# Up products of the MLP: the first pass by twos, and sums of token blocks in the order of their products, with a fourth sum buffer

## The chip, the cores and the metric

The kernel runs on one core of one Trainium2 chip. The metric is the device time of one execution in microseconds (us): the median of three runs of the kernel before is 2343.8 us (2342.3 to 2343.92). One more execution was taken with the hardware profiler; all rows of the trace come from it.

## The reference, cut to what matters

A decoder trunk of two layers on 1024 tokens of width 1024, in float32. Each layer has a token mixer (attention in layer 0, a gated recurrence in layer 1) and then a channel mixer. The change is in the first product of the channel mixer, `h @ w1`, in both layers.

```python
D_MODEL = 1024; SEQ = 1024; DEPTH = 2; D_FF = 4 * D_MODEL

def sq_relu_mlp(h, w1, w2):
    a = jax.nn.relu(h @ w1)
    return (a * a) @ w2
...
    for layer in range(DEPTH):
        ...
        h = h + rms_norm(m, norm_gains[layer, 1])
        a = rms_norm(h, norm_gains[layer, 2])
        h = h + rms_norm(sq_relu_mlp(a, mlp_w1[layer], mlp_w2[layer]), norm_gains[layer, 3])
    return h
```

## The kernel before, in words

**Products.** Every float32 factor is split (`split`, L74) into a high half, made by a copy on ACT (L76), and a low half, the remainder, made by a subtraction on DVE (L77). One step of a product is then three matmuls (`mm3`, L81 to L83): high by high, high by low, low by high. The third is the first that reads the low half of the weights. One product of the up stage (`product`) takes 512 of the 1024 features, 128 columns of w1 and 512 tokens: four steps, 12 matmuls.

**The up stage (`mlp_up`).** Features and tokens are cut in two, so the activations are four blocks: B11 and B21 (first 512 tokens; first and second half of the features), B12 and B22 (last 512 tokens). In the code they are `A[0, 0]`, `A[1, 0]`, `A["whole"]` and `A[1, 1]`; in the order of instructions A00, A10, whole (in layer 1 a part of acc) and A11. The 4096 columns of w1 go in 16 blocks p of 256, two halves of 128 each. With a scheme of Strassen's kind a block needs seven products instead of eight. Two are of B11 and B21 and add up in one PSUM bank. The other five (`others`) are, in the order of the code, of T2, T1, T3, B22 and T4, where T1 to T4 are sums of the four blocks: T1 = B12 - B11, T2 = B22 - T1, T3 = B22 - B12, T4 = B21 - T2. Their weights are sums of w1's quarters: wS12 (`w_parts(s12)`; for T2 and T1), wS34 (for T3 and B22), and wb, the plain quarter, for T4.

**The first pass.** For the first eight blocks (`EARLY`) the products of B11 and B21 need only the first 512 tokens. They run while the last tokens still come out of the mixer and are transposed by PE into B12 and B22 (`into_features`, L176). The pass is the loop at L861: weights are loaded and split, B11's product goes to a PSUM bank, ACT copies it out (`first_two`, L805, to a tile he; called sP1), B21's product is added in the same bank (`add_second`), ACT takes relu (L797) and square (L798). sP1 and the result h11 are stored in DRAM by POOL's queue (L865, L794) and loaded again by SP (L875, L877) when `others` reaches the block. There are two banks for this (pool PG, tag mm) and two tiles he.

**The sums.** `tsums` (L726) makes T1 to T4 on DVE in two halves of the features, k = 0 and k = 2. A half has eight sums and four splits, so there are 16 sums and 8 splits of 128x1024 in all; the high half of each split is a copy on ACT. A half needs three buffers s, and there are three. `others` uses two of the same buffers for each block (s12 and s34).

**Results.** Each block adds its products into tiles of 128x512 that rotate through a ring (`h512`): two he, NH of tag h, and NM of tag h2, which lie where `A["whole"]` was, so that they exist only after the sums have read it. A tile comes free when its store to DRAM has landed or its last reader is done. The ring has 13 tiles in layer 0 (NH 7, NM 4) and 14 in layer 1 (NH 4, NM 8).

**Order.** The code is recorded and a scheduler writes each engine's instructions in one fixed order when the program is built; `tc.high_priority(offset=AHEAD[layer])` lets the first pass go ahead of what stands before it in the code. At run time each engine goes through its list and waits for semaphores; nothing overtakes.

Of the kernel before, what the change touches and what calls it, by code (L numbers as in the profile page):

```python
# [11 lines left out]
F32 = mybir.dt.float32  # L12
# [4 lines left out]
ALU = mybir.AluOpType  # L17
# [4 lines left out]
P = 128  # L22
# [17 lines left out]
EARLY = 8  # L40
# [18 lines left out]
def trunk(ctx, tc, x, x_t, positions, norm_gains, mla_w_in, mla_q_norm, mla_kv_norm, mla_w_uq, mla_w_ukv, mla_w_o,  # L59
          hgrn_w_in, hgrn_lb_logits, hgrn_o_norm, hgrn_w_o, mlp_w1, mlp_w2, out):  # L60
    nc = tc.nc
    PE, ACT, DVE, POOL, SP = nc.tensor, nc.scalar, nc.vector, nc.gpsimd, nc.sync

    def pool(stack, name, bufs=1, side=None, **kw):
        return stack.enter_context(tc.tile_pool(name=name, bufs=bufs, side=side, reuse_waits="tile", **kw))
# [3 lines left out]
    def new(p, shape, dt, tag, bufs=None):  # L69
        uid[0] += 1  # L70
        kw = {} if bufs is None else {"bufs": bufs}
        return p.tile(shape, dt, tag=tag, name=f"{tag}_{uid[0]}", **kw)

    def split(dst, src):  # L74

        ACT.activation(dst[:, 0], src, AF.Copy)  # L76
        DVE.tensor_tensor(dst[:, 1], src, dst[:, 0].bitcast(F32), ALU.subtract)  # L77
# [7 lines left out]
    x = x[0]  # L85
# [15 lines left out]
    first = new(const, [P, 1], F32, "first")  # L101
# [523 lines left out]
    q, qstack = mla()  # L625
# [79 lines left out]
    def mlp_up(layer):  # L705
# [3 lines left out]
        w1 = mlp_w1[layer].rearrange("(k p) c -> p k c", p=P)  # L709
        with tc.tile_pool(name=f"up{layer}", bufs=1, side="left", reuse_waits="tile") as wp:  # L710

            NH, NM = (7, 4) if layer == 0 else (4, 8)
            new(wp, [P, 512], F32, "h", NH)
            new(wp, [P, 1024], F32, "s", 3)
            T2 = new(wp, [P, 2, 4, 512], F32R, "T2")
            T3 = new(wp, [P, 2, 4, 512], F32R, "T3")
            T4 = new(wp, [P, 2, 4, 512], F32R, "T4")
# [5 lines left out]
            def f32(x):  # L723
                return x.bitcast(F32)

            def tsums():  # L726

                for k in range(0, 4, 2):
                    def part(X, i):
                        return f32(X[:, i, k:k + 2])  # L730

                    def tmp():
                        return new(wp, [P, 1024], F32, "s", 3).rearrange("p (k c) -> p k c", c=512)

                    a, b, c = tmp(), tmp(), tmp()

                    b12 = B12[:, :, k:k + 2].rearrange("p t k q -> p k t q")

                    def by_tile(x):
                        return x.rearrange("p k (t q) -> p k t q", q=P)  # L740

                    DVE.tensor_tensor(by_tile(b), b12, by_tile(part(B11, 0)), ALU.subtract)
                    DVE.tensor_tensor(b, b, part(B11, 1), ALU.subtract)
                    d = c
                    DVE.tensor_tensor(d, part(B22, 0), b, ALU.subtract)
                    DVE.tensor_tensor(d, d, part(B22, 1), ALU.add)
                    split(T2[:, :, k:k + 2], d)
                    DVE.tensor_tensor(by_tile(a), by_tile(part(B22, 0)), b12, ALU.subtract)
                    DVE.tensor_tensor(a, a, part(B22, 1), ALU.add)
                    split(T1[:, :, k:k + 2], b)  # L750
                    split(T3[:, :, k:k + 2], a)
                    e = d
                    DVE.tensor_tensor(e, part(B21, 0), d, ALU.subtract)
                    DVE.tensor_tensor(e, e, part(B21, 1), ALU.add)
                    split(T4[:, :, k:k + 2], e)

            def product(ps, w, X, more=False):

# [6 lines left out]

            def h512():
                tag = ring[hs["n"] % len(ring)]
                hs["n"] += 1
                p, bufs = {"he": (G, 2), "h": (wp, NH), "h2": (hs["more"], NM)}[tag]
                return new(p, [P, 512], F32, tag, bufs)  # L770

            def raw_early(p):

                own["n"] += 1
                r = new(G0 if own["n"] % 2 else G, [P, 1024], F32, "raw").rearrange("p (k c) -> p k c", c=P)
                SP.dma_start(r, w1[:, :, p * 256:p * 256 + P])
                return r
# [7 lines left out]
            def w_parts(src):  # L785
                own["w"] = own.get("w", 0) + 1
                w = new(G0, [P, 2, 1024], F32R, "w", 1) if own["w"] % 5 == 0 else new(G, [P, 2, 1024], F32R, "w", 4)
                n = src.shape[1] * src.shape[2]
                v = w[:, :, :n].rearrange("p i (k c) -> p i k c", c=src.shape[2])
                split(v, src)  # L790
                return v
# [8 lines left out]
            def first_two(p, wa):  # L800

                a = new(PG, [P, 512], F32, "mm")
                product(a, wa, B11)
                sP1 = h512() if p >= EARLY else new(G, [P, 512], F32, "he", 2)
                ACT.activation(sP1, a, AF.Copy)  # L805
                return a, sP1

            def add_second(p, a, w12):
                product(a, w12[:, :, :, :P], B21, True)
                h11 = h512() if p >= EARLY else new(G, [P, 512], F32, "he", 2)  # L810
                act2(h11, a)
                spill(0, p, h11)
                return h11

            def others(p, rA, rB, wb, sP1, h11, second=None):
                s12 = new(wp, [P, 1024], F32, "s", 3).rearrange("p (k c) -> p k c", c=256)
                s34 = new(wp, [P, 1024], F32, "s", 3).rearrange("p (k c) -> p k c", c=256)
                DVE.tensor_tensor(s12[:, :, :P], rA[:, :, P:], rB[:, :, P:], ALU.add)
                DVE.tensor_tensor(s12[:, :, P:], s12[:, :, :P], rA[:, :, :P], ALU.subtract)
                wS12 = w_parts(s12)  # L820
                DVE.tensor_tensor(s34[:, :, :P], rA[:, :, :P], rA[:, :, P:], ALU.subtract)
                DVE.tensor_tensor(s34[:, :, P:], rB[:, :, :P], s12[:, :, P:], ALU.subtract)
                b = new(PG, [P, 512], F32, "tr")
                product(b, wS12[:, :, :, P:], T2)
                U = h512()
                DVE.tensor_tensor(U, b, sP1, ALU.add)
                if second is not None:
                    h11 = second()
                wS34 = w_parts(s34)
                c = new(PM, [P, 512], F32, "mm")  # L830
                product(c, wS12[:, :, :, :P], T1)
                X5 = h512()
                DVE.tensor_tensor(X5, c, U, ALU.add)
                d = new(PM, [P, 512], F32, "c")
                product(d, wS34[:, :, :, :P], T3)
                h22 = h512()
                DVE.tensor_tensor(h22, d, X5, ALU.add)
                product(c, wS34[:, :, :, P:], B22, True)
                h12 = X5
                DVE.tensor_tensor(h12, c, U, ALU.add)  # L840
                product(d, wb, T4, True)
                h21 = U
                DVE.tensor_tensor(h21, d, U, ALU.add)
                for h in (h22, h12, h21):
                    act2(h, h)
                spill(3, p, h22)
                s1 = h512()
                DVE.tensor_tensor(s1, h12, h22, ALU.add)
                spill(4, p, s1)
                s2 = h512()  # L850
                DVE.tensor_tensor(s2, s1, h11, ALU.subtract)
                spill(5, p, s2)
                s3 = h12
                DVE.tensor_tensor(s3, h11, h12, ALU.subtract)
                spill(6, p, s3)
                spill(1, p, h21)
                s4 = h512()
                DVE.tensor_tensor(s4, h21, s2, ALU.subtract)
                spill(2, p, s4)

            for p in range(EARLY):  # L861
                with tc.high_priority(offset=AHEAD[layer]):
                    w12 = w_parts(raw_early(p))
                    a, sP1 = first_two(p, w12[:, :, :4])
                    POOL.dma_start(psp[p * P:(p + 1) * P, :], sP1)  # L865
                    add_second(p, a, w12[:, :, 4:])
            tsums()

            act["whole"].close()
            hs["more"] = pool(act["stack"], f"more{layer}", side="right")  # L870
            for p in range(NP):
                rA, rB = raw_half(p, 0), raw_half(p, 1)
                if p < EARLY:
                    h11 = h512()
                    SP.dma_start(h11, hsp[0, p * P:(p + 1) * P, :])  # L875
                    sP1 = h512()
                    SP.dma_start(sP1, psp[p * P:(p + 1) * P, :])  # L877
                    others(p, rA, rB, w_parts(rB[:, :, P:]), sP1, h11)
                else:
                    a, sP1 = first_two(p, w_parts(rA[:, :, :P]))  # L880
                    wb = w_parts(rB)
                    others(p, rA, rB, wb[:, :, :, P:], sP1, None, lambda: add_second(p, a, wb))
# [487 lines left out]
```

## Time and profile before

| | us |
|---|---|
| median of 3 runs | 2343.8 |
| lowest, highest | 2342.3, 2343.92 |
| profiled execution, its own time | 2346.75 |
| span of the profiled execution, first to last instruction | 2345.1 |
| PE busy in it | 2266.8 (97%) |
| DVE, ACT, POOL busy | 1596.5, 1169.4, 346.9 |

The profiled execution took 2.95 us more than the median of the runs. Start times in the rows are from the start of the span. A row of a timeline names the engine, the line, the operation, what it writes and reads, and, where the engine was idle before it, for how long and who ended the idle time. Matmuls overlap: one row of 0.39 us starts some 0.23 us after the one before it, so the pace is read from the starts. PEclk is the granted clock of the tensor engine as a share of full speed.

### The profile page before, as it was taken

The numbers are of one execution on the slowest core, as the hardware profiler recorded it, in microseconds if no ns is written. First come the engines' busy times: TensorE is split into PE (matmuls) and PEld (weight loads), VectorE is DVE, ScalarE is ACT, GpSimd is POOL, SyncE is SP. The second block draws the span as 40 slices with busy tenths as digits, with TensorE's granted clock in tenths as the row PEclk, the third lists the DMA queues.
The fourth block names the chain that finished last, engine by engine and source line by source line (L and its number), as shares of the span: only waits on it lengthen the run. The fifth ranks groups of instructions, "written<-read, shape, count | busy, mean of one in ns | idle before, by whom it ended". The sixth has DMA issues, their size and how long they took to land. (4 is left out here: it accounts for less than half of the span.)

```text
span 2345.1 us, 30698 instructions
## 1 busy us (share of the span) xinstructions
PE 2266.8 (97%) x11487; PEld 1910.8 (81%) x11487; DVE 1596.5 (68%) x2287; ACT 1169.4 (50%) x1893; POOL 346.9 (15%) x718
## 2 busy tenths in 40 slices
PE   8999999989999999999999999999979999999998
PEld 8789998867778878888788888888767788788886
DVE  5658885378766556588655767756778766466696
ACT  5445655364445444445565546755454445444343
POOL 1300000021212100001322213212221222100001
PEclk9999999999999999999999999999999999999999
DMA  7010002465644484565612333222346544663664
GB/s 220 24 32 10 10 10 79 146 211 189 210 157 166 159 299 135 180 229 175 198 46 82 110 102 121 82 81 70 108 165 220 182 164 149 210 240 120 217 216 159
DMA packets 229283, 333.12 MB, mean 142 GB/s; under 512 B 16743, under 2 KB 136590, under 8 KB 229134
## 3 DMA queue, kind: packets, MB, share of 16 engines
q1 hardware_dynamic: 205326, 251.45, 33.4%
q0 software_dynamic: 23808, 79.71, 9.1%
q8 instruction: 90, 1.47, 0.3%
q14 instruction: 59, 0.48, 0.1%
HBM read 247.22 MB, written 83.89 MB: 141 GB/s over the span
## 5 line engine op out<-in xcount | busy, mean ns | idle before, releaser
L77 DVE TENSOR_TENSOR w<-raw,w 128x1024 fp32r<-128x1024 f32 (+1 forms) x240 | 278.1, 1163 | 185.2 <-ACT w L76 184.2
L76 ACT ACTIVATE w<-raw 128x1024 fp32r<-128x1024 f32 (+1 forms) x240 | 237.8, 997 | 239.2 <-PE mm L83 119.6
L81 PE MATMUL mm<-A,w 128*128 128x512 f32 x832 | 331.2, 399 | 23.4 <-ACT he L797 12.2
L82 PE MATMUL mm<-A,w 128*128 128x512 f32 x832 | 327.6, 395 | 0.6 <-DVE A L77 0.6
L76 ACT ACTIVATE w<-s 128x1024 fp32r<-128x1024 f32 x156 | 165.3, 1060 | 321.8 <-PE c L83 118.5
L83 PE MATMUL mm<-A,w 128*128 128x512 f32 x832 | 325.5, 393 | 0.0
L77 DVE TENSOR_TENSOR w<-s,w 128x1024 fp32r<-128x1024 f32 x156 | 190.5, 1222 | 143.9 <-ACT w L76 143.8
L81 PEld LDWEIGHTS mm<-A,w 128*128 128x128 f32 x832 | 157.7, 190 | 64.5 <-ACT he L797 15.7
L145 POOL TENSOR_TENSOR rstd<-rstd,nhalf 128x1 f32<-128x1 f32 x56 | 44.4, 794 | 959.1 <-DVE rstd L144 934.2
L83 PEld LDWEIGHTS mm<-A,w 128*128 128x128 f32 x832 | 157.6, 190 | 33.1
L82 PEld LDWEIGHTS mm<-A,w 128*128 128x128 f32 x832 | 157.8, 190 | 32.2 <-DVE A L77 1.0
L82 PE MATMUL mm<-w,w 128*128 128x512 f32 x432 | 168.7, 391 | 1.0 <-DVE w L77 0.9
L83 PE MATMUL mm<-w,w 128*128 128x512 f32 x432 | 168.3, 390 | 0.0
L81 PE MATMUL mm<-w,w 128*128 128x512 f32 x432 | 154.4, 392 | 3.2 <-ACT u L1015 2.0
L794 POOL DMA_DIRECT2D hsp<-h x177 | 95.4, 540 | 388.8 <-ACT h L798 208.7
L81 PE MATMUL mm<-w,A 128*128 128x256 f32 (+2 forms) x352 | 111.5, 319 | 4.2 <-ACT A L76 3.5
L83 PE MATMUL mm<-w,A 128*128 128x256 f32 (+2 forms) x352 | 110.9, 316 | 0.0
L82 PE MATMUL mm<-w,A 128*128 128x256 f32 (+2 forms) x352 | 110.2, 314 | 0.0
L81 PE MATMUL c<-T,w 128*128 128x512 f32 x256 | 99.6, 389 | 0.0
L82 PE MATMUL c<-T,w 128*128 128x512 f32 x256 | 99.6, 389 | 0.0
L83 PE MATMUL c<-T,w 128*128 128x512 f32 x256 | 99.3, 389 | 0.0
L81 PEld LDWEIGHTS mm<-w,w 128*128 128x128 f32 x432 | 80.8, 188 | 22.6 <-ACT u L1015 2.9
(443 smaller groups left out, 5641.2 us busy)
## 6 DMA issues: line engine op xcount, KB each, us to landing
raw<-in_mlp_w_dram SPq DMA_DIRECT2D x92, 512.0 KB, 4.3
hsp<-h POOLq DMA_DIRECT2D x177, 256.0 KB, 2.9
s<-in_mlp_w_dram SPq DMA_DIRECT2D x80, 512.0 KB, 6.2
raw<-hsp SPq DMA_DIRECT2D x76, 512.0 KB, 4.0
raw<-in_hgrn_w_in_dram SPq DMA_DIRECT2D x64, 512.0 KB, 4.2
sx<-hsp SPq DMA_DIRECT2D x36, 512.0 KB, 3.9
hsp<-he POOLq DMA_DIRECT2D x47, 256.0 KB, 2.8
xt<-in_x_dram SPq DMA_DIRECT2D x16, 512.0 KB, 5.5
```

Of the source, the lines that this page charges most:

```text
L76: ACT.activation(dst[:, 0], src, AF.Copy)
L77: DVE.tensor_tensor(dst[:, 1], src, dst[:, 0].bitcast(F32), ALU.subtract)
L81: PE.matmul(ps, lhs[0], rhs[0], start=start, stop=False, skip_group_check=more)
L82: PE.matmul(ps, lhs[0], rhs[1], start=False, stop=False, skip_group_check=more)
L83: PE.matmul(ps, lhs[1], rhs[0], start=False, stop=stop, skip_group_check=more)
L145: POOL.tensor_tensor(r, r, nhalf[:, :1], ALU.pow)
L794: POOL.dma_start(hsp[i, p * P:(p + 1) * P, :], h)
```

## The change

Three edits in `mlp_up`. The first pass goes by pairs of blocks: both B11 products, then both B21 products. `tsums` is cut in two functions: `tsums12` makes T2 and T1 of both halves, and `tsums34` makes T4 of both halves and then T3 of both; the second is handed to `others` of block 0 as `then` and is recorded between the split of wS12 and the sums of s34. For that the sums of T2 live on, and there is a fourth buffer s; NH is two smaller in both layers, so the ring has 11 and 12 tiles.

```diff
-            NH, NM = (7, 4) if layer == 0 else (4, 8)
+            NH, NM, NS = (5, 4, 4) if layer == 0 else (2, 8, 4)
             new(wp, [P, 512], F32, "h", NH)
-            new(wp, [P, 1024], F32, "s", 3)
+            new(wp, [P, 1024], F32, "s", NS)
...
+            t2s = {}
+
+            def tsums12():
+                for k in (0, 2):
+                    b, d = tmp(), tmp()
+                    DVE.tensor_tensor(by_tile(b), b12(k), by_tile(part(B11, 0, k)), ALU.subtract)
+                    DVE.tensor_tensor(b, b, part(B11, 1, k), ALU.subtract)
+                    DVE.tensor_tensor(d, part(B22, 0, k), b, ALU.subtract)
+                    DVE.tensor_tensor(d, d, part(B22, 1, k), ALU.add)
+                    split(T2[:, :, k:k + 2], d)
+                    split(T1[:, :, k:k + 2], b)
+                    t2s[k] = d
+
+            def tsums34():
+                for k in (0, 2):
+                    e = t2s[k]
+                    DVE.tensor_tensor(e, part(B21, 0, k), e, ALU.subtract)
+                    DVE.tensor_tensor(e, e, part(B21, 1, k), ALU.add)
+                    split(T4[:, :, k:k + 2], e)
+                for k in (0, 2):
+                    a = tmp()
+                    DVE.tensor_tensor(by_tile(a), by_tile(part(B22, 0, k)), b12(k), ALU.subtract)
+                    DVE.tensor_tensor(a, a, part(B22, 1, k), ALU.add)
                     split(T3[:, :, k:k + 2], a)
...
-            def others(p, rA, rB, wb, sP1, h11, second=None):
-                s12 = new(wp, [P, 1024], F32, "s", 3).rearrange("p (k c) -> p k c", c=256)
-                s34 = new(wp, [P, 1024], F32, "s", 3).rearrange("p (k c) -> p k c", c=256)
+            def others(p, rA, rB, wb, sP1, h11, second=None, then=None):
+                s12 = new(wp, [P, 1024], F32, "s", NS).rearrange("p (k c) -> p k c", c=256)
                 DVE.tensor_tensor(s12[:, :, :P], rA[:, :, P:], rB[:, :, P:], ALU.add)
                 DVE.tensor_tensor(s12[:, :, P:], s12[:, :, :P], rA[:, :, :P], ALU.subtract)
                 wS12 = w_parts(s12)
+                if then is not None:
+                    then()
+                s34 = new(wp, [P, 1024], F32, "s", NS).rearrange("p (k c) -> p k c", c=256)
...
-            for p in range(EARLY):
+            for p in range(0, EARLY, 2):
+
                 with tc.high_priority(offset=AHEAD[layer]):
-                    w12 = w_parts(raw_early(p))
-                    a, sP1 = first_two(p, w12[:, :, :4])
-                    POOL.dma_start(psp[p * P:(p + 1) * P, :], sP1)
-                    add_second(p, a, w12[:, :, 4:])
-            tsums()
-
-            act["whole"].close()
-            hs["more"] = pool(act["stack"], f"more{layer}", side="right")
+                    w12, first = {}, {}
+                    for i in (p, p + 1):
+                        w12[i] = w_parts(raw_early(i))
+                        first[i], sP1 = first_two(i, w12[i][:, :, :4])
+                        POOL.dma_start(psp[i * P:(i + 1) * P, :], sP1)
+                    for i in (p, p + 1):
+                        add_second(i, first[i], w12[i][:, :, 4:])
+            tsums12()
+
+            def rest():
+                tsums34()
+
+                act["whole"].close()
+                hs["more"] = pool(act["stack"], f"more{layer}", side="right")
+
...
-                    others(p, rA, rB, w_parts(rB[:, :, P:]), sP1, h11)
+                    others(p, rA, rB, w_parts(rB[:, :, P:]), sP1, h11, then=rest if p == 0 else None)
```

The number of instructions is the same on every engine, and outside the two up stages their order is the same. PE around the last eight transposes of layer 0 (tr_848 and tr_849, which complete B12 and B22), before; mm_871 and mm_881 are the banks of blocks 2 and 4:

```order
L82 MATMUL mm_871_5159<-A10_749_4344,w_870_5156 128x512
L83 MATMUL mm_871_5159<-A10_749_4344,w_870_5156 128x512
L176 MATMUL tr_848_5053<-ident_6_65,y_842_5034 128x128 x4
L176 MATMUL tr_849_5059<-ident_6_65,y_842_5034 128x128 x4
L81 MATMUL mm_881_5233<-A00_748_4343,w_880_5230 128x512
L82 MATMUL mm_881_5233<-A00_748_4343,w_880_5230 128x512
```

The same place on PE after the change; mm_885 is the bank of block 5:

```order
L82 MATMUL mm_885_5254<-A00_748_4343,w_884_5251 128x512
L83 MATMUL mm_885_5254<-A00_748_4343,w_884_5251 128x512
L176 MATMUL tr_848_5053<-ident_6_65,y_842_5034 128x128 x4
L176 MATMUL tr_849_5059<-ident_6_65,y_842_5034 128x128 x4
L81 MATMUL mm_881_5233<-A10_749_4344,w_880_5230 128x512
L82 MATMUL mm_881_5233<-A10_749_4344,w_880_5230 128x512
```

Before, seven products stood ahead of these transposes (B11 of blocks 0 to 3, B21 of 0 to 2); now ten do (B11 of blocks 0 to 5, B21 of 0 to 3). In layer 1 it is nine before and ten now.

ACT in the last third of layer 0's first pass, before (he are sP1 and h11, mm their banks, T1 the high half of a sum):

```order
L805 ACTIVATE he_887_5283<-mm_886_5270 128x512
L798 ACTIVATE he_883_5261<-he_883_5261 128x512
L76 ACTIVATE T1_858_5079<-s_903_5396 128x1024
L797 ACTIVATE he_888_5298<-mm_886_5270 128x512
L805 ACTIVATE he_892_5320<-mm_891_5307 128x512
L798 ACTIVATE he_888_5298<-he_888_5298 128x512
```

And the two last pairs after it; L814 is now the copy, L806 the relu, L807 the square, w_909 is wS12 of block 0:

```order
L814 ACTIVATE he_892_5320<-mm_891_5307 128x512
L76 ACTIVATE T1_858_5079<-s_901_5386 128x1024
L814 ACTIVATE he_896_5341<-mm_895_5328 128x512
L806 ACTIVATE he_897_5356<-mm_891_5307 128x512
L807 ACTIVATE he_897_5356<-he_897_5356 128x512
L76 ACTIVATE T2_854_5075<-s_902_5387 128x1024
L806 ACTIVATE he_898_5372<-mm_895_5328 128x512
L76 ACTIVATE w_909_5410<-s_908_5407 128x1024
```

Before, the copy of a bank, L805, and its relu, L797, stand three places apart, and the copy of the next block's bank follows the relu directly; now the copies of two banks come first and the two relus after them. The high half of wS12 stands behind the last relu.

DVE between the sums and the two weight splits of block 0 in layer 0, before (w_912 is wS12, w_915 is wS34):

```order
L77 TENSOR_TENSOR T3_855_5076<-s_902_5395,T3_855_5076 128x1024
L754 TENSOR_TENSOR s_904_5397<-s_904_5397,A10_749_4344 128x1024
L77 TENSOR_TENSOR w_912_5433<-s_910_5429,w_912_5433 128x1024
L821 TENSOR_TENSOR s_911_5430<-raw_905_5418 128x4x128
L822 TENSOR_TENSOR s_911_5430<-raw_906_5420,s_910_5429 128x4x128
L77 TENSOR_TENSOR T4_856_5077<-s_904_5397,T4_856_5077 128x1024
L77 TENSOR_TENSOR w_915_5453<-s_911_5430,w_915_5453 128x1024
```

And after (w_909 is wS12; w_915 is wS34 as before):

```order
L77 TENSOR_TENSOR w_909_5410<-s_908_5407,w_909_5410 128x1024
L77 TENSOR_TENSOR T4_856_5077<-s_900_5377,T4_856_5077 128x1024
L756 TENSOR_TENSOR s_902_5387<-A10_749_4344,s_902_5387 128x1024
L77 TENSOR_TENSOR T3_855_5076<-s_910_5421,T3_855_5076 128x1024
L761 TENSOR_TENSOR s_911_5426<-A11_750_4345,whole_751_4349 128x1024
L757 TENSOR_TENSOR s_902_5387<-s_902_5387,A10_749_4344 128x1024
L832 TENSOR_TENSOR s_912_5435<-raw_903_5396 128x4x128
L833 TENSOR_TENSOR s_912_5435<-raw_904_5398,s_908_5407 128x4x128
L762 TENSOR_TENSOR s_911_5426<-s_911_5426,A11_750_4345 128x1024
L837 TENSOR_TENSOR h_914_5451<-tr_913_5438,he_906_5402 128x512
L77 TENSOR_TENSOR T4_856_5077<-s_902_5387,T4_856_5077 128x1024
L77 TENSOR_TENSOR w_915_5453<-s_912_5435,w_915_5453 128x1024
```

The low half of wS12 moved ahead of seven of the sums' instructions; the low half of wS34 is still behind all of them but one, the last split of T3. In DVE's list there are, from the first sum to the low half of wS12, 17 instructions of 1024 elements and 3 of 512, and to the low half of wS34 25 and 6. Layer 1 has the same list.

## Rows read from the trace of the kernel before

**Rows 1.** The page: busy time of each engine, share of the span, instructions.

```profile
PE 2266.8 (97%) x11487; PEld 1910.8 (81%) x11487; DVE 1596.5 (68%) x2287; ACT 1169.4 (50%) x1893; POOL 346.9 (15%) x718
```

**Rows 2.** PE's waits, first pass, layer 0 (481.5 to 543.1): sum, count, longest.

```profile
PE mm L81 <- ACT he L797: 6.0, 6, 2.3
PE mm L81 <- ACT he L805: 3.4, 2, 2.2
```

**Rows 3.** PE's waits in the first pass, layer 1 (1693.6 to 1751.7).

```profile
PE mm L81 <- ACT he L797: 6.1, 5, 2.2
PE mm L81 <- ACT he L805: 1.2, 1, 1.2
```

**Rows 4.** Timeline of PE in layer 0's first pass: start, duration, engine, line, idle before.

```profile
481.56 0.71 PE L81 MATMUL mm<-A,w 128*128 128x512 f32 x2
...
491.24 0.79 PE L81 MATMUL mm<-A,w 128*128 128x512 f32 x1 [2.19 <-ACT he L805]
...
510.45 1.03 PE L176 MATMUL tr<-ident,y 128*128 128x128 f32 x8
...
520.26 0.50 PE L81 MATMUL mm<-A,w 128*128 128x512 f32 x1 [2.26 <-ACT he L797]
...
523.13 0.39 PE L81 MATMUL mm<-A,w 128*128 128x512 f32 x1
...
525.62 0.39 PE L83 MATMUL mm<-A,w 128*128 128x512 f32 x1
```

**Rows 5.** Busy time by stretch: us, engines, granted clock, DMA share, GB/s.

```profile
core 0: us, PE busy (x) PEld busy (x) DVE busy (x) ACT busy (x) POOL busy (x), PEclk, DMA share, GB/s
491.20:494.70 3.50, 3.46 (x8) 2.78 (x9) 3.41 (x6) 1.45 (x3) 1.15 (x2) 0.51 0.89 313
```

**Rows 6.** Timeline of ACT before PE's restart at 497.48.

```profile
495.88 1.06 ACT L76 ACTIVATE w<-raw 128x1024 fp32r<-128x1024 f32 x1 [3.23 <-PE mm L83]
496.84 0.58 ACT L797 ACTIVATE he<-mm 128x512 f32<-128x512 f32 x1
```

**Rows 7.** Timeline of DVE, layer 0: first sum, pace, a half-width sum, low half of wS34.

```profile
512.89 1.22 DVE L742 TENSOR_TENSOR s<-whole,A 128x1024 f32<-128x1024 f32 x1
...
517.01 1.22 DVE L748 TENSOR_TENSOR s<-A,whole 128x1024 f32<-128x1024 f32 x1
518.15 1.22 DVE L77 TENSOR_TENSOR T<-s,T 128x1024 fp32r<-128x1024 f32 x1
...
538.58 0.68 DVE L818 TENSOR_TENSOR s<-raw,raw 128x512 f32<-128x512 f32 x1
...
547.48 1.22 DVE L77 TENSOR_TENSOR w<-s,w 128x1024 fp32r<-128x1024 f32 x1
```

**Rows 8.** Timeline of PE, layer 0: third matmul of block 0's T3 product.

```profile
550.32 0.39 PE L83 MATMUL c<-T,w 128*128 128x512 f32 x1
```

**Rows 9.** Timeline of PE, layer 1: first pass, T2 product, T3 product's third matmul.

```profile
1693.63 0.50 PE L81 MATMUL mm<-A,w 128*128 128x512 f32 x1 [0.22 <-DVE acc L1298]
...
1757.33 0.79 PE L81 MATMUL tr<-T,w 128*128 128x512 f32 x1 [5.37 <-ACT w L76]
...
1765.43 0.39 PE L83 MATMUL c<-T,w 128*128 128x512 f32 x1
```

**Rows 10.** Timeline of ACT, layer 1: a copy to he that waits for a store.

```profile
1727.26 0.60 ACT L805 ACTIVATE he<-mm 128x512 f32<-128x512 f32 x1 [1.62 <-DMA hsp<-he]
```

**Rows 11.** Timeline of DVE, layer 1: first sum, low half of wS34.

```profile
1729.02 1.22 DVE L742 TENSOR_TENSOR s<-acc,A 128x1024 f32<-128x1024 f32 x1
...
1761.92 1.23 DVE L77 TENSOR_TENSOR w<-s,w 128x1024 fp32r<-128x1024 f32 x1
```

**Rows 12.** PE's longest group of waits after block 0, layer 0 (557.5 to 805).

```profile
PE mm L81 <- DVE h L833: 2.6, 2, 2.0
```

**Rows 13.** PE's longest group of waits after block 0, layer 1 (1768 to 2032).

```profile
PE tr L81 <- DVE he L826: 3.1, 1, 3.1
```

**Rows 14.** Timeline of DVE, layer 0: a result that waits for a reload.

```profile
617.12 0.69 DVE L826 TENSOR_TENSOR h<-tr,h 128x512 f32<-128x512 f32 x1 [1.53 <-DMA h<-psp]
```

More of the change, by code (lines that the diff above doesn't have):

```diff
@@ L724, in f32, with tmp @@
                 return x.bitcast(F32)
[L726 to L746, printed above, removed]
+            def tmp():
+                return new(wp, [P, 1024], F32, "s", NS).rearrange("p (k c) -> p k c", c=512)
@@ new lines, in part, with by_tile, b12 @@
+            def part(X, i, k):
+                return f32(X[:, i, k:k + 2])
+            def by_tile(x):
+                return x.rearrange("p k (t q) -> p k t q", q=P)
+            def b12(k):
+                return B12[:, :, k:k + 2].rearrange("p t k q -> p k t q")
+            t2s = {}
[6 more added lines that the diff above has]
+                    DVE.tensor_tensor(d, d, part(B22, 1, k), ALU.add)
@@ L747, in tsums @@
                     split(T2[:, :, k:k + 2], d)
-                    DVE.tensor_tensor(by_tile(a), by_tile(part(B22, 0)), b12, ALU.subtract)
-                    DVE.tensor_tensor(a, a, part(B22, 1), ALU.add)
                     split(T1[:, :, k:k + 2], b)
+                    t2s[k] = d
[9 more added lines that the diff above has]
+                    DVE.tensor_tensor(a, a, part(B22, 1, k), ALU.add)
@@ L751, in tsums @@
                     split(T3[:, :, k:k + 2], a)
[L752 to L755, printed above, removed]
             def product(ps, w, X, more=False):
@@ L767, in h512 @@
                 tag = ring[hs["n"] % len(ring)]
+                assert tag != "h2" or hs["more"]
                 hs["n"] += 1
```

## The prediction

> **What bounds the kernel now.** I read the busy times first. The tensor engine is busy 97% of the span [rows 1], so only its idle time and the stretches in which it runs at its lower clock can be won. Next come PE's waits inside the two first passes. They are 6.0 and 3.4 us in layer 0 [rows 2], 6.1 and 1.2 in layer 1 [rows 3], and both groups wait for ACT, which is half idle on average. ACT's timeline tells why: a split of weights stood 3.23 us waiting for PE, and the relu that frees the bank stood behind it [rows 6]. PE in turn waits for this relu before it can put B11 of the next block but one in the same bank.
>
> Then the sums. In layer 0 the first of them starts at 512.89, after the last transposes at 510.45 [rows 4], and the low half of wS34 starts at 547.48 and lasts 1.22 us [rows 7]: a chain of 35.8 us on DVE. The third matmul of T3's product, the first reader of that low half, starts at 550.32 [rows 8]. In layer 1 the chain goes from 1729.02 to 1763.15 [rows 11] and that matmul starts at 1765.43 [rows 9]. From here on block 0 is in both kernels the same work, so the gain of a layer is by how much earlier this matmul comes, less what the later blocks lose.
>
> Last the clock. After a wait of 2.19 us that ended at 491.24 [rows 4], PE got 0.51 of its clock from 491.20 to 494.70 and began 8 matmuls there in 3.50 us [rows 5]. At the full pace, (525.62 - 523.13)/11 = 0.2265 us a matmul [rows 4], 8 take 1.8. So one such stretch costs 1.7 us. Another wait of 2.26 us, ended at 520.26, left the pace after it at the full one [rows 4]: a wait of this size lowers the clock sometimes.
>
> **The pairs, layer 0.** They add and remove no instruction. What goes is the wait for relu right behind B21: between B21 of a block and the next product in its bank stands B21 of the other block, 12 x 0.2265 = 2.72 us, while the relu takes 0.58 [rows 6] and the split ahead of it 1.06. I cost the waits that remain before the last transposes at 0.7 us, near the smallest of what shows now; at none it would be 0, at the size of layer 1's copy wait 1.2 [rows 3].
>
> But the list also puts three more products ahead of the last transposes, ten for seven. PE starts at 481.56 [rows 4]. Ten products are 27.2 us; three earlier groups of eight transposes are 0.9 each by their pace (the row of the last group shows 1.03 for eight, with the last one's tail [rows 4]), 2.7. That gives 481.56 + 27.2 + 2.7 + 0.7 = 512.2 for the start of the last group against 510.45, and 513.1 for its end. The copies out of PSUM and the start of the sums took 1.5 us from there before (510.45 + 0.9 to 512.89); by 1.0 to 1.5 the first sum is now at about 514.1, 1.2 later. Six products remain, so the first pass ends near 513.1 + 16.3 = 529.4.
>
> **The sums, layer 0.** DVE's pace is 1.137 us for 1024 elements (517.01 to 518.15) and about 0.60 for 512, the 0.68 less the overlap [rows 7]. To the end of the low half of wS12 are 17 wide instructions and 3 narrow: 514.1 + 19.3 + 1.8 = 535.2. To that of wS34 are 25 and 6: 514.1 + 28.4 + 3.6 = 546.1. Today's chain takes 35.8 for what by the same prices is about 32, because DVE waits for ACT's halves of the T splits; I take 32.0, since the relus and copies of the first pass, behind which those halves stand, no longer wait for PE. At worst the 35.8 stays.
>
> So T2's product starts when ACT has done the high half of wS12, which now stands behind the last relu: 529.4 plus a relu and a split (0.58 + 1.06 [rows 6]) and their hand-overs, 531.8. Its third matmul waits for 535.2. T2 and T1 are done near 540, T3 begins near 544, and its third matmul comes at 546.3. The stall thus isn't removed, it is moved: PE is through the first pass early and then idles some 11 us in four pieces of 2.3 to 3.6. The gain of layer 0 is 550.32 - 546.3 = 4.0.
>
> **Layer 1.** Ten products stand ahead of the last transposes where there were nine. 1693.63 [rows 9] + 27.2 + 2.7 = 1723.5, transposes to 1724.4, first sum about 1725.3. It was at 1729.02 [rows 11]; today a copy on ACT stood 1.62 us waiting for the store of an older he [rows 10], and PE waits of 7.3 [rows 3] lay ahead. The same 32.0 us end at 1757.3, and T3's third matmul comes at 1757.4: 1765.43 - 1757.4 = 8.0. The 5.37 us idle before T2's product [rows 9] is partly inside this.
>
> **The clock.** The first passes lose their waits and so perhaps their slow stretches, but four new waits of over 2 us stand behind each. By the two cases in rows 4 I take one slow stretch in two layers: 1.7 lost. Bounds: none, or 1.7 in each layer, 3.4.
>
> The Trainium skill, in "TensorE: Matmul & The Clock Gate", section "Part 1: The HAM clock gate (the "warmup" mystery)", says that the throttled state is the default, that an idle engine falls back to half of 2.4 GHz and that activity releases it. The stretch at 0.51 agrees; the wait that ended at 520.26 shows no fall. Were the fall certain after the new waits, both layers would pay, 1.7 us more than in my sum, and the gain would be 7.6.
>
> **The ring.** The tiles for results go from 13 to 11 and from 14 to 12 in both layers' remaining 15 blocks. Today the longest group of waits there is 2.6 us in layer 0, longest 2.0 [rows 12], and 3.1 in layer 1 [rows 13]; a reload waits up to 1.53 [rows 14]. PE is otherwise dense there, and a stored tile is taken again one or two blocks later, so I take 1.0 us for both layers. Bounds: 0.5 won (as noise in order) and 20 lost, ten waits of 2.0. The fourth s buffer itself costs nothing in time: the sums of T2 only live longer.
>
> **Sum.** 4.0 + 8.0 - 1.7 - 1.0 = 9.3. The profiled execution took 2346.75, 1.65 more than its span and 2.95 more than the median of 2343.8. On the profiled basis it is 2337.45, on the median 2334.5, which I predict. In its own case the time is 2327 to 2339: the upper end with both slow stretches and 1.5 more for the ring and the chain, the lower with none and the chain started 1.5 us earlier in each layer.
>
> **Rivals.** *A, all waits go.* If the sums didn't bind, the gain is the waits, 9.4 + 7.3, plus two slow stretches, 3.4, plus the idle 5.4: about 26, 2318. For it: that idle is really there now. Against: 25 wide and 6 narrow instructions can't be shorter than 32 us at the pace of rows 7. Chance 0.10, mostly for the sums starting earlier than I have them.
>
> *B, the chain keeps its waits.* If DVE still needs 35.8 and 34.1 us, T3's third matmul comes at 550.1 and 1759.5: gains of 0.2 and 5.9. Less two slow stretches, 3.4, and the ring, 1.0, a gain of 1.7 is left: 2342.1. For it: ACT's list around the sums still mixes splits, copies and relus, and the high halves of T1 and T2 stand behind copies that need PE. Against: nothing on ACT there waits long once PE doesn't. Chance 0.17; this is also where the change as a whole does nothing that can be told.
>
> *C, the smaller ring.* With fewer tiles the sum of a block waits for a store or a reload, DVE holds the bank, and PE stands. The price is up to 2.0 us each [rows 12], in 30 blocks. From (10.3 + 4.7)/2.0, between seven and eight such waits, the kernel is slower by more than can be told; ten of them make 2343.8 - 10.3 + 20 = 2353.5. For it: waits on that ring exist with 13 tiles already. Against: they are few, two or three a layer. Chance 0.12.
>
> **How the numbers follow.** Mine has 0.61, A 0.10, B 0.17, C 0.12. 0.2%, 4.7 us, is about what a measurement of this kernel can tell from no change. Faster by more is mine but for its upper edge, 0.57, and A, 0.10: 0.67. Within it: B and that edge, 0.21. Slower: C, 0.12. The range 2323 to 2347 leaves out most of A and C, about 0.2.
>
> **What would show it.** Right: PE's waits for relu in the first pass are gone or under 1 us each; the first sum comes about 1.2 us later in layer 0 and 3.7 earlier in layer 1; PE idles four times between the first pass and T3, ended by the weight split of DVE or ACT; T3's third matmul comes 4.0 and 8.0 us earlier; the waits of later blocks stay within a few us. Wrong: a chain on DVE of over 34 us (B), no idle before T3 (A), PE waiting again and again for sums of later blocks, with DVE or a DMA on the ring ahead of them (C), or the pairs merely moving the wait from relu to the copy of a bank.

## The result, and the profile after

The changed kernel takes 2333.31 us (median of 4 runs, 2331.1 to 2336.08) against 2343.86 for the kernel before: a ratio of 0.9948, interval 0.9933 to 0.9962, 10.5 us less. On a second chip it was 2334.91 against 2346.91, 0.9953 (0.9940 to 0.9965). The forecast was 2334.5. The time is right, but the terms that made it are not: the gains of the two layers came out at about half or less, and the smaller ring, which I had as a loss, is the biggest gain. The experiments below show by how much.

PE does the same work [rows 1], in a span of 2333.7 us (page of the changed kernel; engine, busy us, share, instructions):

```profile
PE 2266.3 (97%) x11487; PEld 1912.8 (82%) x11487; DVE 1595.5 (68%) x2287; ACT 1170.1 (50%) x1893; POOL 346.1 (15%) x718
```

The waits of the two first passes, of 9.4 and 7.3 us [rows 2, 3], shrank. First layer 0 (482.5 to 533.4), then layer 1 (1690.5 to 1740.3); columns: sum, count, longest.

```profile
PE mm L81 <- ACT he L814: 1.5, 1, 1.5
PE mm L82 <- DVE A L77: 0.6, 1, 0.6
PE mm L81 <- ACT he L806: 0.2, 1, 0.2
...
PE mm L81 <- ACT he L814: 1.3, 1, 1.3
PE mm L81 <- ACT he L806: 0.4, 1, 0.4
```

L814 is the copy, L806 the relu. So the relu is off the path as forecast, and a copy that stands in the same way costs 1.5 us once. PE's timeline in layer 0, the counterpart of [rows 4, 8]: start of the pass, last transposes, T2's first and third matmul, T3's first and third.

```profile
482.52 0.48 PE L81 MATMUL mm<-A,w 128*128 128x512 f32 x1
...
516.16 1.03 PE L176 MATMUL tr<-ident,y 128*128 128x128 f32 x8
...
535.19 0.50 PE L81 MATMUL tr<-T,w 128*128 128x512 f32 x1 [1.63 <-ACT w L76]
...
538.89 0.80 PE L83 MATMUL tr<-T,w 128*128 128x512 f32 x1 [2.49 <-DVE w L77]
...
546.86 0.50 PE L81 MATMUL c<-T,w 128*128 128x512 f32 x1 [0.67 <-ACT w L76]
...
549.78 0.50 PE L83 MATMUL c<-T,w 128*128 128x512 f32 x1 [2.18 <-DVE w L77]
```

The waits are the four forecast, ended by the splits that the forecast named (on ACT or DVE), 7.0 us together instead of 11. The chain on DVE that ends the last of them (counterpart of [rows 7]):

```profile
517.52 1.23 DVE L745 TENSOR_TENSOR s<-whole,A 128x1024 f32<-128x1024 f32 x1 [1.83 <-ACT whole L178]
...
548.51 1.21 DVE L77 TENSOR_TENSOR w<-s,w 128x1024 fp32r<-128x1024 f32 x1
```

549.72 - 517.52 = 32.2 us; the forecast had 32.0. But it begins 35.0 us behind the pass's start, where the forecast had 514.1 - 481.56 = 32.5: 2.5 us late. In layer 1 (counterpart of [rows 9, 11]):

```profile
1690.54 0.48 PE L81 MATMUL mm<-A,w 128*128 128x512 f32 x1
...
1758.52 0.50 PE L83 MATMUL c<-T,w 128*128 128x512 f32 x1 [2.18 <-DVE w L77]
...
1726.26 1.23 DVE L745 TENSOR_TENSOR s<-acc,A 128x1024 f32<-128x1024 f32 x1 [3.17 <-ACT acc L178]
...
1757.25 1.22 DVE L77 TENSOR_TENSOR w<-s,w 128x1024 fp32r<-128x1024 f32 x1
```

From the pass's first matmul to T3's third it took 68.76 and 71.80 us before [rows 4, 8, 9]; now it is 549.78 - 482.52 = 67.26 and 67.98. That is 1.5 and 3.8 us won where the forecast had 4.0 and 8.0, and 5.3 of a span shorter by 11.4. Where is the rest? The table follows the same six places in PE's list (the 2752nd, 3036th, 4301st, 8768th, 9041st and 10301st of 11487; before they start at 481.56, 559.31, 853.43, 1693.63, 1771.08 and 2066.75) through all profiles. Discarded matmuls of an experiment are left out of the count.

| stretch, us | up to layer 0's pass | first pass and block 0 | rest of up 0, start of down 0 | to layer 1's pass | first pass and block 0 | rest of up 1, start of down 1 |
|---|---|---|---|---|---|---|
| before | 479.2 | 77.7 | 294.1 | 840.2 | 77.4 | 295.7 |
| changed | 480.2 | 76.9 | 292.8 | 838.3 | 74.9 | 289.9 |
| changed, again | 478.4 | 75.8 | 294.7 | 839.8 | 73.7 | 289.8 |
| pairs | 478.2 | 76.9 | 291.8 | 839.2 | 76.4 | 294.5 |
| sums | 478.5 | 76.3 | 291.0 | 839.7 | 77.4 | 287.2 |
| ring | 478.4 | 79.5 | 292.3 | 838.8 | 74.9 | 287.1 |
| ring_l0 | 480.5 | 81.3 | 292.9 | 840.4 | 77.8 | 295.8 |
| ring_l1 | 479.3 | 77.0 | 291.8 | 838.7 | 74.6 | 286.9 |
| ring13 | 479.0 | 77.8 | 292.0 | 841.3 | 78.0 | 289.6 |
| ring11 | 479.1 | 75.7 | 295.9 | 841.4 | 74.9 | 298.8 |
| pairs_l1 | 479.3 | 75.6 | 293.3 | 841.5 | 76.1 | 286.5 |
| w34 | 479.4 | 76.6 | 290.6 | 839.7 | 76.0 | 286.8 |
| warm | 479.6 | 76.8 | 291.7 | 839.9 | 75.0 | 286.1 |
| warm34 | 478.7 | 78.2 | 290.6 | 838.6 | 76.6 | 287.2 |

From the end of the last column to the last matmul it is 269.1 us in every profile. The first and fourth columns hold work that no kernel changes; they spread over 2.3 and 3.2 us, so a difference of 2 or 3 us between two single profiles shows nothing, and only what repeats counts. One difference does: the last column is 294.5 to 295.8 in the three kernels with 14 tiles in layer 1's ring and 286.1 to 289.9 in the eight with 12. This is the biggest piece of the gain, 5.8 us in the changed kernel, and the experiments put it down to the edit that I had costed as a loss.

### The profile page after: what moved, and what is told of

Its sections match the earlier page's. It is cut to its first block, busy times and chain, and to the rows that moved or that the text cites. A ratio compares the mean times of both kernels' runs of the same rounds, so it can differ in the third digit from the quotient of the medians.

```text
span 2333.7 us, 30701 instructions
## 1 busy us (share of the span) xinstructions
PE 2266.3 (97%) x11487; PEld 1912.8 (82%) x11487; DVE 1595.5 (68%) x2287; ACT 1170.1 (50%) x1893; POOL 346.1 (15%) x718
## 5 line engine op out<-in xcount | busy, mean ns | idle before, releaser
L82 PEld LDWEIGHTS mm<-A,w 128*128 128x128 f32 x832 | 157.4, 189 | 32.5 <-DVE A L77 1.0
```

Source lines behind the costliest of these rows:

```text
L82: PE.matmul(ps, lhs[0], rhs[1], start=False, stop=False, skip_group_check=more)
```

## The experiments

**Each part alone.** "pairs" is the kernel before with the new loop of the first pass; "sums" the changed kernel with the old loop; "ring" the kernel before with two tiles less in both layers, and nothing else:

```diff
-            NH, NM = (7, 4) if layer == 0 else (4, 8)
+            NH, NM = (5, 4) if layer == 0 else (2, 8)
```

> The kernel before with the first pass by pairs alone (old order of the sums, three buffers s, ring of 13 and 14). Theory 1 (the chain of sums on DVE from the last transposes to block 0's weights sets the end, the pairs set where it begins): in layer 0 ten products now stand ahead of the last transposes, the first sum is 4 to 5 us later, at 517 to 518, the low half of wS12 comes 28 us later, T2's third matmul near 545 to 546, T3's third near 551: a gain of -1 to 0 there; in layer 1 T3's third at 1757 to 1759, from a start of the pass that is the same as before's, a gain of 6 to 8. In all 5 to 8 us faster than before, 2336 to 2339. Rival 1 (the gain is the PE waits of the first pass, the sums do not matter): all of the 10.5 us of the whole change, 2333. Rival 2 (the pairs only move the wait to T2, the sums are the gain): 2342 to 2345.

> The changed kernel with the first pass one block at a time as before (sums in the new order, fourth s buffer, ring of 11 and 12). Theory 1: the first pass keeps its waits of 9 and 7 us and ends at 543 and 1752; T2 of block 0 can begin at once in both layers; T3's third matmul is 1 us earlier in layer 0 and 3 to 5 us in layer 1. In all 4 to 6 us faster, 2338 to 2340, less up to 1 for the ring. Rival 1 (the PE waits are the gain): 2343 to 2345. Rival 2 (the sums are the gain): 2333 to 2335.

> The kernel before with the ring of results cut to 11 and 12 tiles and nothing else (the memory of two tiles stays unused). My sum had 1.0 us lost by it: 2344 to 2346. The rival with many more waits for stores and reloads: 2352 or more. If tiles do not matter at all: 2343 to 2344.5.

Measured: pairs 2343.62 (ratio 0.9993, 0.9982 to 1.0005), sums 2335.69 (0.9966, 0.9953 to 0.9980), ring 2334.38 (0.9957, 0.9945 to 0.9969), with 2344.09 before. The pairs alone win nothing that can be told, where theory 1 had 5 to 8 us and rival 1 all of it. By these two numbers rival 2 would stand, the sums as the gain; but "sums" has the smaller ring in it, and the smaller ring alone wins 9.7 us, nearly as much as the whole change, where I had a loss of 1. So all three fall as the cause of the gain. What the pairs and the sums add to the ring, 10.5 us against 9.7, is within the noise. With the pairs alone the waits for the relu are gone, but PE then stands 10.96 and 12.97 us ahead of block 0's T2 product, until ACT has split wS12.

**Which layer's ring, and is less better?** A new theory 2: the size of the ring moves places in the lists that are written at build time. The kernels are the one before with other NH: ring_l1 (7 in layer 0, 2 in layer 1), ring_l0 (5, 4), ring13 (7, 3), ring11 (7, 1).

> The kernel before with the ring cut in layer 1 alone, from 14 tiles to 12. Theory 2 (the ring's size moves places in the written lists; with 14 tiles PE comes in layer 1 to a T2 product of a block whose weight split on ACT can begin only when the matmul right ahead has been done, and U's sum stands behind it on DVE; with 12 there is no such place in layer 1): nearly the whole gain of the smaller ring, 7 to 9 us, 2335 to 2337, and no wait over 1 us on PE in layer 1 after block 0. Rival 4 (the gain is layer 0's): 2343 to 2345.

> The kernel before with the ring cut in layer 0 alone, from 13 tiles to 11. Theory 2: the list of layer 0 has such a place with either ring, and layer 1 keeps its own: 2342 to 2345, within 0.1% of the kernel before. Rival 4 (the gain is layer 0's): 2334 to 2337.

> The kernel before with 13 tiles in layer 1 instead of 14 (layer 0 as it was). Its lists have one such place in layer 1, in an earlier block, and none of those at the end of the stage. Theory 2: one wait of 1 to 3 us on PE, perhaps with a stretch at half clock, 2337 to 2341. Rival 3 (fewer tiles are faster by themselves, evenly): between 14 and 12 tiles, 2339 to 2340, without such a wait.

> The kernel before with 11 tiles in layer 1 instead of 14 (layer 0 as it was). Its lists have four such places in layer 1, after block 0, and one more where a sum on DVE stands right ahead. Theory 2: waits of 1 to 3 us at each, with stretches at half clock behind some: slower than with 12 tiles by 4 to 10 us, 2340 to 2347. Rival 3 (fewer tiles are faster by themselves): faster than with 12, 2329 to 2334.

Measured, with 2345.82 before: 14 tiles cut to 12 in layer 1 alone 2330.93 (0.9936, 0.9923 to 0.9948); layer 0 alone 2345.15 (0.9993, 0.9982 to 1.0004); 13 tiles 2341.07 (0.9980, 0.9968 to 0.9991); 11 tiles 2347.74 (1.0009, 1.0000 to 1.0017). So the ring's gain is layer 1's, and it is no matter of fewer tiles: 11 are slower than 12 by 0.7%. Rivals 3 and 4 fall. Theory 2 had the order of the four and their signs; the effect is larger at both ends than I wrote (2330.93 for 2335 to 2337, 2347.74 for 2340 to 2347), and the other two lie just above their ranges (2345.15 for 2342 to 2345, 2341.07 for 2337 to 2341). The stretches at half clock that I had expected behind waits in ring11 did not come: its granted clock was 1.00 behind the longest of them, 3.10 us, from 1847.27 to 1850.70. PE's waits in layer 1 after block 0 tell the same; first ring_l0, which has 14 tiles there as the kernel before [rows 13]:

```profile
PE tr L81 <- DVE he L826: 3.1, 1, 3.1
PE mm L81 <- ACT u L1015: 1.1, 1, 1.1
PE mm L81 <- DVE h L833: 1.0, 2, 0.6
PE mm L82 <- DVE w L77: 0.9, 1, 0.9
PE mm L81 <- ACT w L76: 0.7, 1, 0.7
```

Then ring_l1, 12 tiles, which has this wait alone:

```profile
PE mm L82 <- DVE w L77: 0.7, 1, 0.7
```

And the longest of ring11:

```profile
PE tr L81 <- DVE h L826: 3.1, 1, 3.1
PE tr L81 <- ACT w L76: 2.3, 2, 1.1
PE c L83 <- DVE w L77: 1.5, 1, 1.5
```

The wait of 3.1 us in ring_l0, engine by engine (timelines):

```profile
1846.57 0.39 PE L83 MATMUL mm<-A,w 128*128 128x512 f32 x1
1850.06 0.47 PE L81 MATMUL tr<-T,w 128*128 128x512 f32 x1 [3.10 <-DVE he L826]
...
1846.99 1.06 ACT L76 ACTIVATE w<-s 128x1024 fp32r<-128x1024 f32 x1 [2.05 <-PE mm L83]
...
1848.08 1.23 DVE L77 TENSOR_TENSOR w<-s,w 128x1024 fp32r<-128x1024 f32 x1 [2.07 <-ACT w L76]
1849.22 0.68 DVE L826 TENSOR_TENSOR he<-tr,h 128x512 f32<-128x512 f32 x1
```

ACT's split of the next weights begins when the matmul right ahead has been done; DVE's half of it waits for ACT; and the sum U, of T2's product and sP1 (L826), which must empty the bank that PE wants next, stands behind that on DVE, though its own product ended long before. In DVE's list with 14 tiles these two stand in this order (w_2601 is wS12 of the block that waits, 2567 the U of an earlier block):

```
L77 TENSOR_TENSOR w_2601_16052<-s_2599_16048,w_2601_16052 128x1024
L826 TENSOR_TENSOR he_2567_15844<-tr_2566_15831,h2_2561_15817 128x512
```

With 12 tiles U falls on another tile, and its sum stands 14 places ahead of w_2601's split instead of one behind; on PE that T2 product begins 24 matmuls later. The wait is there in before, pairs and ring_l0, at 3.1 us each time, and in no kernel with 12 tiles. Behind it lay a stretch at the lower clock; in before (third last column):

```profile
1846.30:1849.80 3.50, 3.50 (x10) 2.75 (x9) 2.90 (x5) 1.13 (x2) 0.00 (x0) 0.51 0.82 310
```

By its clock this stretch costs 3.50 x 0.49 = 1.7 us. PE's waits in the last column sum to 6.8 us in ring_l0 and 0.7 in ring_l1, so the two together make 7.8 of the 8.9 us between these kernels. The sum of the waits follows the table in the others too: 2.6 us with 13 tiles, 10.2 with 11, at most 1.0 in all other kernels with 12. The changed kernel has 3.3, and so it wins less in this column than the ring alone, 5.8 us against 8.6:

```profile
PE mm L81 <- DVE h L844: 1.3, 1, 1.3
PE tr L83 <- DVE w L77: 1.3, 1, 1.3
PE mm L82 <- DVE w L77: 0.7, 1, 0.7
```

That the order of the lists is the cause is read from these waits and lists at four sizes of the ring; no run changes the order with 14 tiles kept.

The ring's size tells in the fifth column as well. With the old loop and the old sums T3's third matmul of layer 1 comes 71.8 to 72.8 us behind the pass's start with 13 or 14 tiles (before, ring_l0, ring13) and 69.4 to 69.7 with 11 or 12 (ring, ring_l1, ring11): a wait for the relu in the middle of the pass is 2.17 to 2.65 us in the first three and 0.73 to 0.99 in the others. So some of what layer 1 won up to T3 may be the ring's too; what does it was not looked into. And layer 0's 1.5 us up to T3 is not clear of chance: ring_l1, ring13 and ring11, which leave layer 0 as it was, take 68.0, 69.1 and 66.6 us there, before 68.8, the changed kernel 67.3 and 66.5.

**The chain, and the idle time.** On the changed kernel: "w34" writes block 0's part on DVE as T4 of the first half, s34, split of wS34, T3 of the first half, T4, T3 of the second; "warm" adds discarded matmuls to the waits ahead of T2's and T3's third; "warm34" is w34 with the first ten of these; pairs_l1 is ring_l1 with the new loop.

```diff
+                def keep(w):
+                    for n in range(10):
+                        PE.matmul(d, w[:, 0, n % 4, :P], B11[:, 0, n % 4], start=True, stop=True)
```

> The changed kernel with 10 matmuls whose result is thrown away ahead of T2's third matmul of block 0, and 10 more ahead of T3's first one, in both layers, where PE idles 2.7 us and 0.8 + 2.3 us. They add 20 x 0.2265 = 4.5 us of work a layer, nearly all in idle time. If the stretches at half clock that follow this idle time (12 matmuls in 4.30 us instead of 2.72 from 551.08 in layer 0, 17 in 5.60 instead of 3.85 from 1758.52 in layer 1) come from the idle time, they go: 1.6 and 1.75 us won, less up to 0.5 of matmuls that do not fit: 2330 to 2331. If the clock falls there whatever PE does: the same or up to 1 us slower than the changed kernel, 2333 to 2335.

> The changed kernel with the list on DVE changed for block 0: sums and split of wS34 directly after T4 of the first half, before T3 and before T4 of the second half (the same instructions). Theory 1 (the chain on DVE sets when T3 can begin): the low half of wS34 comes 8 us earlier, the wait ahead of T3's third matmul (2.2 us in both layers) and the one ahead of T3's first (0.7 and 1.0) go, the third matmul starts 3 us earlier in each layer than from the same start now, and the time falls by 4 to 6 us against the changed kernel. If other waits take their place (T3's second half is later by the same list): 0 to 2 us.

> The same with 10 matmuls whose result is thrown away ahead of T2's third matmul of block 0 in both layers. They lie in the wait of 2.6 us that stays there. If the stretch at half clock behind that wait (10 matmuls of T2 in 4.4 us instead of 2.3) is now on the path: 2 to 3 us less a layer than without them at most, 0 to 2 where T3's second half is late anyway. 1 to 5 us faster in all than the kernel without them, and never slower by more than 1.

> The kernel before with layer 1's ring cut to 12 tiles and with the first pass by pairs (old order of the sums). If the pairs only move the wait from the relu to T2 of block 0 (theory 1 by its profiles so far): within 2 us of the kernel with the short ring alone, which took 2330.9: 2329 to 2333. If the PE waits of the first pass are worth their sum where nothing else disturbs (rival 1): 7 to 9 us faster than that, 2322 to 2324.

> The changed kernel itself once more, beside the others on this chip: 2331 to 2336. Its waits after block 0 and the four waits between the first pass and T3 have to be where they were, if they come from the written lists; the place and number of stretches at half clock may differ.

Measured: warm 2331.26 (0.9944, 0.9932 to 0.9956) with 2344.09 before. With 2346.91 before: w34 2331.82 (0.9939, 0.9926 to 0.9951), warm34 2333.21 (0.9942, 0.9930 to 0.9955), pairs_l1 2334.93 (0.9950, 0.9936 to 0.9963), and the changed kernel again 2334.91.

w34 is 3 us faster than that by the medians (the intervals overlap), but not by its mechanism: the table has 76.6 and 76.0 for its first stretches, no less than the changed kernel's. The low half of wS34 came at 537.47, and another wait took its place (w34: DVE's split, then PE's waits from 532 to 557):

```profile
537.47 1.22 DVE L77 TENSOR_TENSOR w<-s,w 128x1024 fp32r<-128x1024 f32 x1
PE c L81 <- ACT T L76: 4.4, 1, 4.4
PE tr L81 <- ACT w L76: 2.9, 2, 1.6
PE tr L83 <- DVE w L77: 1.5, 1, 1.5
```

T3 itself is now what T3's product waits for. DVE has the same sums to make before it, so the order among them moves the wait but does not take it away. What w34 won is again in later lists: its last column is 286.8, the changed kernel's 289.9. warm34 came out 1.4 us slower than w34, where I had expected 1 to 5 faster; the intervals overlap.

warm tests the clock, whose stretches in the changed kernel are (granted clock in the third last column):

```profile
538.89:543.33 4.44, 4.44 (x11) 3.47 (x12) 4.44 (x5) 0.00 (x0) 0.00 (x0) 0.50 0.22 59
551.08:555.38 4.30, 4.30 (x14) 3.39 (x13) 3.48 (x5) 1.06 (x1) 0.00 (x0) 0.62 0.08 19
1747.63:1752.06 4.43, 4.43 (x10) 3.46 (x11) 4.43 (x5) 0.00 (x0) 0.00 (x0) 0.50 0.20 63
1759.34:1762.74 3.40, 3.40 (x10) 2.65 (x9) 3.37 (x6) 0.10 (x1) 0.00 (x0) 0.51 0.00 0
```

The same places in warm, with its second ten discarded matmuls in the middle row:

```profile
537.12:540.40 3.28, 3.01 (x13) 2.18 (x12) 3.28 (x4) 0.78 (x1) 0.00 (x0) 1.00 0.33 85
546.56:550.54 3.98, 3.98 (x10) 3.13 (x11) 3.98 (x5) 1.69 (x2) 0.00 (x0) 0.57 0.71 241
551.01:556.03 5.02, 5.02 (x24) 4.13 (x22) 3.88 (x6) 1.06 (x1) 0.00 (x0) 1.00 0.36 99
```

With the first wait filled the clock stays full behind it, so the idle time did cause the fall at this place. But nothing is won: the next matmul that needs wS34, whose high half ACT must make first, starts 64.6 us behind the pass's start (546.56 - 481.92), in the changed kernel 64.3 (546.86 - 482.52). PE only waits longer for it, 3.73 us, and behind this wait the second ten run at half clock. They put T3's third matmul 2.3 us later (69.55 us behind the pass's start for 67.26), and the full clock after it gives that back. The table's second stretch takes 76.8 us, the changed kernel's 76.9. warm's time, 2331.26, is near the 2330 to 2331 that I expected, but its 2 us, too, lie in the last column.

pairs_l1 is 4 us slower than ring_l1 by the medians, where I expected within 2; the intervals overlap, and its columns differ by no more than columns without any change do. It shows no gain from the pairs, which speaks against rival 1 once more. What layer 0's ring of 11 costs beside 13 (ring against ring_l1, 3.5 us by medians from two chips) is not settled either. The fastest median, ring_l1's 2330.93, is one number changed in the kernel before; by the intervals it can't be told from the changed kernel.

## Why the prediction was right, and where its reasons were wrong

- **What bounds the pass.** Right: the relu behind a split was PE's wait, and by pairs it went, to 0.2 and 0.4 us. That the sums hold PE up next, so that the stall is moved and not removed, was right too, and more than I said: pairs alone win nothing.
- **Gain of layer 0, 4.0, and of layer 1, 8.0.** Mis-sized: 1.5 and 3.8, and 2.3 and 5.0 in the second profile (66.47 and 66.78 us from the pass's start to T3's third). The chain's length was right, 32.2 and 32.2 for 32.0. The step that failed is its start. In layer 0 I had allowed 0.7 us for waits before the last transposes; they were 2.3 in the list above, and every restart costs a little more (the first matmul behind the wait at 535.19 takes 0.34 us to the next start, not 0.23), so the last transposes start 33.6 us after the pass instead of 30.6. In layer 1 I had allowed nothing for such waits; they were 1.7, and the last transposes start 32.5 us after the pass instead of 29.9. There the first sum is 35.7 us behind the pass's start, as before (35.4), not 31.7: for the rest, a copy on ACT still stands before it and waits for a store, as in [rows 10], now 2.10 us:

```profile
1725.15 0.60 ACT L814 ACTIVATE he<-mm 128x512 f32<-128x512 f32 x1 [2.10 <-DMA hsp<-he]
1725.64 0.59 ACT L178 ACTIVATE acc<-tr 128x512 f32<-128x512 f32 x1
```

- The prediction names that wait as part of the old start and leaves it out of the new one. Its one word on it, against rival B, is that nothing on ACT there waits long once PE doesn't; this copy waited for a store, and the change kept that.
- **Clock, -1.7.** Too small: each layer has one stretch at half clock ahead of the wait for wS34, which costs nothing, and one behind T3's third matmul, 12 matmuls in 4.30 us in layer 0 for 2.72, 8 in 3.39 in layer 1 for 1.81. Together 3.2, close to the bound of 3.4: both layers paid. The Trainium skill, in "TensorE: Matmul & The Clock Gate", section "Part 1: The HAM clock gate (the "warmup" mystery)", says that the throttled state is the default and that an idle engine falls back to it; these rows agree, the 1.00 behind ring11's wait of 3.10 us does not.
- **Ring, -1.0.** Wrong in sign: the last column gained 5.8. I treated a ring as a resource, of which less can only cost, and read the waits of [rows 12, 13] as waits for tiles. The 3.1 us of [rows 13] was a place in the list. I had compared the order only around the first pass; the rows of the later blocks would have shown U's sum change its place.
- **Rivals.** A fell: waits of 7.0 us replaced those removed. B, with 0.2 + 5.9 = 6.1 us for the two layers, was the better sum up to T3 (5.3 and 7.3 us measured, 12.0 forecast), but not by its mechanism: the chain took 32.2 us and not 35.8 and 34.1, and it was its start that came late. C had the right place, the blocks after the first, and the wrong sign.

So the time was right by luck: 12.0 - 5.3 = 6.7 us that did not come about met 5.8 + 1.0 = 6.8 us more than forecast in layer 1's later blocks. What is left (1.5 more for the clock; 1.2 by which the second and fifth columns gained more than 5.3 - 3.2, near the 0.98 us that the kernel before waited behind T3's third matmul; and 2.2 won in the first, third and fourth columns together) is within what these columns differ by in kernels that are the same there. With a ring that happened to give a bad list, as 11 tiles in layer 1, the same reasoning would have missed.

## What to carry to other kernels

Where instruction order is fixed at build time, an edit that changes tiles can change the lists far from where it was made: compare the written order over the whole stage, and look on each engine for an instruction that empties a bank but stands behind one that waits for the matmul just ahead. Undo each part alone before believing that a gain is due to the part that was meant to bring it; here the part meant as a price brought the biggest piece. A wait on PE that ends in another engine's chain is not shortened by arriving earlier.

## What the runs showed of the hardware

In the changed kernel the half clock came behind each of four waits, of 2.49, 2.18, 2.56 and 2.18 us (0.50, 0.62, 0.50 and 0.51 in the rows above), and ten discarded matmuls in the first of these kept it at 1.00. But the length of a wait does not settle it. Behind the wait of 3.10 us before the same T2 product, before ran at 0.51 and ring11 at 1.00. In layer 1 of warm34 the clock was 0.51 from 1742.40 to 1745.80, though the ten discarded matmuls ran there, shortly behind a wait of 3.67 us.

And the half clock can cost less than it looks: of 4.44 us at 0.50 in the changed kernel, nothing, because T3's first matmul had to wait for wS34 anyway.
